# Token mixing: the delta rule's keys ahead of the RWKV solve, gates and values placed around the head norms, and modulation products held back

## The chip, the core and the metric

The kernel runs on one core of a Trainium2 chip, as one program. The metric is the device time of one execution in microseconds (us), lower is better. TensorE (PE) multiplies matrices, VectorE (DVE) and ScalarE (ACT) work elementwise, GpSimd (POOL) runs a small triangular inverse, and SyncE (SP) issues nearly all the DMA transfers.

## The reference, cut to what matters

Two streams of 128 tokens (context and latent) go through two layers with the same weights. A layer is a half-step FFN, token mixing, and a second half-step FFN; each of the three is modulated by shift, scale and gate vectors made from a conditioning vector.

```python
def trunk_layer(x, mod, lp, init, ctx_kv, rope):
    m = mod[:, None]
    h = adaln(x, lp["norm_g"][0], m[:, :, 0], m[:, :, 1])
    x = x + 0.5 * m[:, :, 2] * swiglu(h, lp["ffn_w_in"][0], lp["ffn_w_out"][0])
    h = adaln(x, lp["norm_g"][1], m[:, :, 3], m[:, :, 4])
    y, aux = token_mixing(h, lp, init, ctx_kv, rope)
    x = x + m[:, :, 5] * y
    h = adaln(x, lp["norm_g"][2], m[:, :, 6], m[:, :, 7])
    x = x + 0.5 * m[:, :, 8] * swiglu(h, lp["ffn_w_in"][1], lp["ffn_w_out"][1])
    return x, aux
...
def token_mixing(h, lp, init, ctx_kv, rope):
    pa, pb, pc, pd, pg = split_last(h @ lp["w_in"], BLOCK_SIZES)
    y_a, st_a = rwkv7_mixer(pa, lp, init[0])
    y_b, st_b = gla_mixer(pb, lp, init[1])
    y_c, st_c = delta_mixer(pc, lp, init[2])
    ...
    up = jnp.einsum("bsmc,mcd->bsmd", branches, lp["w_branch"])
    gates = jax.nn.sigmoid(pg.reshape(b, s, N_BRANCH, D_MODEL))
    merged = jnp.sum(gates * up, axis=2)
    return merged @ lp["w_out"], (st_a, st_b, st_c, k, v)
```

RWKV and the delta rule are recurrences over the tokens, written as unit-triangular systems of 128 rows for 4 heads, 2 directions and 2 streams. Both end with a norm over the 64 values of each head, as does GLA.

## The kernel before, in words

All weights are float32 and stream from HBM. `wload` brings a piece of up to 512 KB into one of three `raw` buffers (a DMA on SP's queue), and `part` splits each half of it into a high part (`hi`, on ACT) and a low part (`lo = raw - hi`, on DVE), each in one of four buffers. A matrix product is then three fast products: `lo` times the high part of the activations, `hi` times their high part, `hi` times their low part. One split piece of 512 columns feeds 12 TensorE instructions in the mixing, and `block` chains these so that nothing comes between them unless a scheduler needs to.

`mixing` runs the steps that the string `ORDER` names. `b`*mj* is a block: branch *m* (0 RWKV, 1 GLA, 2 delta rule, 3 attention), column block *j* of four. A block is a gate (`gate`: 48 instructions `pg<-h`, four split pieces, then a tanh on ACT) and a value (12 instructions `pu<-yy`, one split piece, which needs the branch's finished output `yy`), then two DVE instructions that multiply and add into `merged` (`mg`). `g2`*j* is a gate of the delta rule's branch alone, kept in an SBUF tile (named g in the trace), and `u2`*j* the value that goes with it. A number behind a colon moves a step ahead in the scheduler's priority. The scheduler sets the final order on every engine; each engine then runs its instructions in that order and waits in place.

The two triangular systems are solved in the same way. A front step fills the system (`SA` for RWKV, `SD` for the delta rule: one tile tag, `S`, with one buffer, so that the second starts when the first is read out). `gather` copies its 32x32 diagonal blocks to `GB` and by DMA to memory (`d<-GB`); `inverse` (`invA`, `invC`) brings them back (`Lb<-d`), inverts them on GpSimd in 62 instructions (`itmp`, `Tb`), and sends the result through memory once more (`d<-Tb`, `TA<-d`); `inverse_out` (`outA`, `outC`) transposes half of it on DVE (`TB<-TA`). `solve`, inside `rwkv_back` and `delta_back`, is four rounds of small TensorE products into `sv` (32 with `TA`, `TB`, then 32 with the system), with ACT or DVE between them, so the scheduler lets gates run in the gaps. `delta_back` then makes the output `yC`, and `headout` norms it: squares on ACT (`hsq`), sums on TensorE (`phs`), a reciprocal root by 11 tiny DVE instructions (`nr`), a broadcast on TensorE (`phr`), then scaling on DVE and the split into `yy`.

`merge_out` splits `merged` into `gg` and multiplies by `w_out` (192 instructions `po<-gg`). The modulation vectors are products `acc<-mraw` (`mod_part`), 64 TensorE instructions in the trace for one vector set; the set for the last gate (`queue_mixing`) is loaded when `u20` starts, into tiles that are free by then, and its products go wherever the scheduler puts them. In the second FFN, `adaln` (`rstd`) squares and sums `xT` (`pss`), takes the root on DVE (`nr`), broadcasts it (`prs`), and makes the next activations `h`.

Of the kernel before, what the change touches and what calls it, by code (L numbers as in the profile page):

```python
# [33 lines left out]
def constants():  # L34
# [52 lines left out]
NEG = CONSTB.shape[1] - 256  # L87


ORDER = """proj_a rwkv_front:-100 proj_t gla_pre proj_d:100 proj_b attention proj_c invA b33 b30 outA rwkv_back:180  # L90
    delta_front invC b31:50 b32 gla:400 b01:-200 b02 b00 b03 b11 b12 b13 b10 outC delta_back g20 g21 u20 g22 u21
    g23 u22:800 u23"""
SPLIT = 40
BLOCK = 1000000
CP = "vavavaavavpa"
# [7 lines left out]
class Net:  # L103
    def __init__(self, ctx, tc, ia, oa, dbg=None):
        self.tc, self.nc, self.ia, self.oa, self.dbg = tc, tc.nc, ia, oa, dbg or {}
        nc = self.nc
        E = ctx.enter_context
        self.cp = E(tc.tile_pool(name="cp", bufs=1))
        self.raw = E(tc.tile_pool(name="raw", bufs=RAW_BUFS))
        self.hl = E(tc.tile_pool(name="hl", bufs=HI_BUFS))  # L110
        self.hp = E(tc.tile_pool(name="hp", bufs=1))
        self.ad = E(tc.tile_pool(name="ad", bufs=1))
        self.sm = E(tc.tile_pool(name="sm", bufs=2))
        self.ps = E(tc.tile_pool(name="ps", bufs=2, space=PSUM))
        self.pw = E(tc.tile_pool(name="pw", bufs=2, space=PSUM))
        self.py = E(tc.tile_pool(name="py", bufs=2, space=PSUM))
        self.mr = None
        self.ch = 0
        self.dr = E(tc.tile_pool(name="dr", bufs=2, space=DRAM))
        cst = self.cp.tile([128, CONSTS.shape[1]], F32, name="cst")  # L120
        self.cst = cst
        self.C = {k: cst[:, o:o + n] for k, (o, n) in COFF.items()}
        self.wg = self.cp.tile([128, CONSTB.shape[1]], BF16, name="wg")
        self.ident = self.C["ident"]
        self.ones = self.cp.tile([128, 128], F32, name="ones")
        nc.gpsimd.memset(self.ones, 1.0)
        self.zb = self.cp.tile([1, 128], BF16, name="zb")
        nc.gpsimd.memset(self.zb, 0.0)
        self.cols = {}
        self.npad = 0  # L130
        self.los = []
        self.pads = [self.ad.tile([128, 2, 2, 130], F32, name=f"pad{i}") for i in range(2)]
        for pad in self.pads:
            nc.gpsimd.memset(pad[:, :, :, 0:1], 0.0)
            nc.gpsimd.memset(pad[:, :, :, 129:130], 0.0)
# [35 lines left out]
    def mm(self, out, lhsT, rhs, start, stop):  # L171
        return self.nc.tensor.matmul(out, lhsT, rhs, start=start, stop=stop)  # L172

    def block(self, mms):


        last = None
        for args in mms:
            self.tc.cur_priority -= BLOCK if last else 0
            i = self.mm(*args)  # L180
            self.tc.cur_priority += BLOCK if last else 0
            if last:
                self.after(i, last)
            last = i

    def tr(self, out, in_):
        p0 = in_.base_partition()
# [42 lines left out]
    def gemm(self, outs, wview, nkc, x, ncol=256, segs=None):  # L230

        nm = (ncol + 127) // 128
        step, sub = 1024 // ncol, 512 // ncol
        wide = isinstance(outs, list)
        for k0 in range(0, nkc, step):
            nk = min(step, nkc - k0)
            if segs is None:  # L240
                srcs = [(0, wview[:, k0:k0 + nk, :])]
            else:
                srcs = [(o, wview[:, k0:k0 + nk, c0:c0 + n]) for o, c0, n in segs]
            part = self.wload(srcs, nk, ncol)
            for kk in range(0, nk, sub):
                n2 = min(sub, nk - kk)
                wh, wl = part(kk, n2)
                mms = []
                for m in range(nm):
                    o = outs[m][:, 0:256] if wide else outs[:, m * 256:(m + 1) * 256]  # L250
                    first, last = (0, nm - 1) if not wide else (m, m)
                    sl = slice(m * 128, (m + 1) * 128)
                    for k in range(n2):
                        kc = k0 + kk + k
                        start, stop = kc == 0 and m == first, kc == nkc - 1 and m == last
                        if wide:
                            two = [(o, wl[:, k, sl], x[:, kc, 0], False, False),
                                   (outs[m].rearrange("p (a t) -> p a t", a=2), wh[:, k, sl], x[:, kc], start, stop)]
                            mms += two[::-1] if start else two
                        else:  # L260
                            mms.append((o, wl[:, k, sl], x[:, kc, 0], start, False))
                            mms.append((o, wh[:, k, sl], x[:, kc, 0], False, False))
                            mms.append((o, wh[:, k, sl], x[:, kc, 1], False, stop))
                self.block(mms)

    def halves(self, out, ps):

# [48 lines left out]
    def mod_part(self, tiles, l, v):  # L316


        w = self.ia["w_mod"][l].rearrange("(k p) c -> p k c", p=128)
        raws, acc = {}, []  # L320

        def load(k):
            raws[k] = tiles()
            c0 = v * 1024
            for t in raws[k]:
                n = t.shape[1]
                self.nc.sync.dma_start(out=t, in_=w[:, k, c0:c0 + n])
                c0 += n

        def prod(k):  # L330
            if k == 0:
                acc.append(self.py.tile([128, 256], F32, tag="y", name="acc"))
            raw = raws.pop(k)
            n = 1024 // len(raw) // 256
            self.block([(acc[0][32 * j:32 * j + 32], self.cT[:, k, :], raw[j // n][:, 256 * (j % n):256 * (j % n) + 256],
                         k == 0, k == 7) for j in range(4)])

        def last():
            row = self.sm.tile([128, 256], F32, tag="mrow", name="modrow", bufs=2)
            self.act(row, acc[0], AF.Copy)  # L340
            p = self.py.tile([128, 256], F32, tag="y", name="acct")
            for c in range(2):
                self.tr(p[:, c * 128:(c + 1) * 128], row[:, c * 128:(c + 1) * 128])

            x = p.rearrange("p (c j e) -> p j c e", c=2, j=4)[:, :, :, 0:2]
            b = self.bm[l][:, 8 * v:8 * v + 8].rearrange("p (j c) -> p j c", j=4).unsqueeze(3)
            o = self.mod[l][:, 8 * v:8 * v + 8, :].rearrange("p (j c) e -> p j c e", j=4)
            for e in range(2):
                self.tt(o[:, :, :, e:e + 1], x[:, :, :, e:e + 1], b, ALU.add)

        return [partial(load, k) for k in range(8)], [partial(prod, k) for k in range(8)] + [last]
# [21 lines left out]
    def flush(self):  # L373

        if self.mr is not None:
            self.fill(len(self.loads), len(self.prods))
            self.mr.close()
            self.mr = None

    def modcols(self, l, i):  # L380

# [157 lines left out]
    def mixing(self, l):  # L539
# [4 lines left out]
        self.mx = self.mr.enter_context(self.tc.tile_pool(name="mx", bufs=1))  # L544
        self.merge_start(l)
        self.first = set(range(4))
        self.g2 = []
        for step in ORDER.split():
            step, _, ahead = step.partition(":")
            ahead = int(ahead or 0)  # L550
# [373 lines left out]
    def rwkv_back(self, l):  # L924
        C = self.C
# [15 lines left out]
                    self.state_out(p, self.oa["o_rwkv"][l, d])  # L941
        self.mm(self.yA, self.zb, self.wg[0:1, 0:512], False, True)

        y = self.t("m1", [128, 512], name="ysA", bufs=2)
        self.act(y, self.yA, AF.Copy)
        p = self.wkt()
        self.mm(p, C["bo"], y, True, True)
# [17 lines left out]
        self.Y[m] = yy  # L965


    def delta_front(self, l):
        nc, ia, C = self.nc, self.ia, self.C
        P, dv = self.P[l]  # L970
        QC = self.QC
# [25 lines left out]
        be = self.t("be", [128, 2, 8])  # L997
# [21 lines left out]
        ev = eg.rearrange("p (d c t) -> p d c t", d=2, c=2)  # L1019
        for d in range(2):  # L1020
            self.tt(EK[:, d], KQ[:, 1], ev[:, d].unsqueeze(2).to_broadcast([128, 2, 2, 128]), ALU.mult)
        self.yC = self.py.tile([128, 512], F32, tag="y", name="yC")
        self.mm(self.yC, self.zb, self.wg[0:1, 0:512], True, False)
        self.SD = SD = self.t("S", [128, 4, 2, 4, 128], name="SD")
# [2 lines left out]
        for s in range(2):  # L1027
# [24 lines left out]
            if s == 1:  # L1052
                for d in range(2):
                    self.gather(SD, d)
            for d in range(2):
                U = UD[:, 2 * d + s].rearrange("p h v -> p (h v)")
                if s == 0:
# [255 lines left out]
    def branch(self, l, m, j, part):  # L1313

        if part == "g":
            if j % 2 == 0:
                self.g2 += [self.t("ab"[j // 2] + "4", [128, 4, 256], name="g2")]
            self.gate(m, j, self.g2[j // 2][:, 2 * (j % 2):2 * (j % 2) + 2])
            return
        if part == "u":  # L1320
            if j == 0:
                self.queue_mixing(l)
            th = self.g2[j // 2][:, 2 * (j % 2):2 * (j % 2) + 2]
        else:
            th = self.t("th", [128, 2, 256], bufs=2)
            self.gate(m, j, th)
# [21 lines left out]
    def merge_out(self, l):  # L1348
# [5 lines left out]
        for k, n in OUT_UNITS:  # L1354
            p = self.mmt("po")
            self.gemm(p, wo[:, :, 128 * k:128 * (k + n)], 8, gg, ncol=128 * n)
            self.residual(p, k, n, ga)


    def finish(self):  # L1360
# [114 lines left out]
```

## Time and profile before

| | |
|---|---|
| median of 3 runs | 1620.99 us (1619.61 to 1624.06) |
| profiled execution | 1624.48 us, its span 1622.7 us |
| mean granted TensorE clock | 0.977 |
| TensorE busy | 1559.8 us, 96% of the span |
| VectorE, ScalarE, GpSimd busy | 1118.9, 871.1, 168.8 us |
| read from HBM | 303.87 MB, 190 GB/s over the span |

The span runs from the first to the last instruction; 1.8 us of the execution lie around it. Matmuls are pipelined, so a busy TensorE is not one at its peak: the start-to-start distances say more. The granted clock is 1.00 at 2.4 GHz and 0.50 at 1.2 GHz, its two levels. The mixing of the first layer lies at about 250 to 625 us, that of the second at about 1045 to 1417 us.

### The profile page before, as it was taken

The numbers are of one execution on the slowest core, as the hardware profiler recorded it, in microseconds if no ns is written. First come the engines' busy times: TensorE is split into PE (matmuls) and PEld (weight loads), VectorE is DVE, ScalarE is ACT, GpSimd is POOL, SyncE is SP. The second block draws the span as 40 slices with busy tenths as digits, with TensorE's granted clock in tenths as the row PEclk, the third lists the DMA queues.
The fourth block names the chain that finished last, engine by engine and source line by source line (L and its number), as shares of the span: only waits on it lengthen the run. The fifth ranks groups of instructions, "written<-read, shape, count | busy, mean of one in ns | idle before, by whom it ended". The sixth has DMA issues, their size and how long they took to land.

```text
span 1622.7 us, 30913 instructions
## 1 busy us (share of the span) xinstructions
PE 1559.8 (96%) x11760; PEld 1335.7 (82%) x11760; DVE 1118.9 (69%) x2478; ACT 871.1 (54%) x1737; POOL 168.8 (10%) x332
## 2 busy tenths in 40 slices
PE   6999999999999989999999999999999988999997
PEld 3888888888878878888878888888887887988886
DVE  4667667777687358777577775777857853877765
ACT  3556556556444346666456665554644443666653
POOL 0000000153018000000000000002800450000000
PEclk9999999999999899999999999999999998999999
DMA  9899776445246445996779867563544562646653
GB/s 341 303 316 314 247 246 200 105 111 150 75 118 190 114 127 180 314 311 199 234 234 317 277 205 227 181 175 79 144 120 117 144 169 66 186 147 188 194 184 115
DMA packets 276996, 310.86 MB, mean 192 GB/s; under 512 B 23792, under 2 KB 254192, under 8 KB 276848
## 3 DMA queue, kind: packets, MB, share of 16 engines
q1 hardware_dynamic: 274832, 302.60, 59.4%
q0 software_dynamic: 1728, 5.24, 1.6%
q8 instruction: 92, 1.51, 0.4%
q10 hardware_dynamic: 288, 1.05, 0.2%
q14 instruction: 56, 0.46, 0.1%
HBM read 303.87 MB, written 4.98 MB: 190 GB/s over the span
## 4 chain that ended last, share of the span: by engine, by line
PE 80%; DVE 7%; POOL 5%; DMA 4%; issue 2%; ACT 2%; SPq 0%; DVEq 0%; ACTq 0%; POOLq 0%
PE pg L172 21%; PE po L172 18%; PE pu L172 16%; PE acc L172 4%; PE wk L172 4%; PE pA L172 4%; PE sv L172 3%; POOL Tb L881 2%; POOL itmp L880 2%; DVE lo L160 2%; PE pT L172 1%; PE yA L172 1%; PE phs L172 1%; DMA TA<-d 1%; PE phr L172 1%
## 5 line engine op out<-in xcount | busy, mean ns | idle before, releaser
L160 DVE TENSOR_TENSOR lo<-raw,hi 128x512 fp32r<-128x512 f32 (+2 forms) x840 | 576.0, 692 | 290.9 <-ACT hi L157 287.0
L157 ACT ACTIVATE hi<-raw 128x512 fp32r<-128x512 f32 (+2 forms) x840 | 520.5, 625 | 451.7 <-PE pg L172 140.1
L172 PE MATMUL pg<-h,hi 128*128 128x256 f32 (+1 forms) x1728 | 444.9, 334 | 6.6 <-DVE h L163 3.6
L172 PE MATMUL pg<-h,lo 128*128 128x256 f32 x1216 | 339.5, 291 | 0.8 <-ACT hi L157 0.5
L172 PEld LDWEIGHTS pg<-h,hi 128*128 128x128 f32 x1728 | 294.6, 194 | 36.3 <-issue 5.4
L172 PEld LDWEIGHTS pg<-h,lo 128*128 128x128 f32 x1216 | 234.8, 193 | 19.9 <-issue 4.9
L172 PE MATMUL po<-zz,hi 128*128 128x512 f32 x704 | 247.5, 396 | 0.0
L172 PE MATMUL pu<-h,hi 128*128 128x512 f32 x704 | 247.4, 396 | 0.0
L172 PE MATMUL po<-zz,lo 128*128 128x256 f32 x704 | 193.1, 282 | 0.0
L172 PE MATMUL pu<-h,lo 128*128 128x256 f32 x704 | 181.6, 278 | 0.0
L172 PEld LDWEIGHTS po<-zz,hi 128*128 128x128 f32 x704 | 130.8, 188 | 30.9 <-issue 0.8
L172 PEld LDWEIGHTS pu<-h,hi 128*128 128x128 f32 x704 | 129.3, 188 | 24.0 <-issue 0.4
L172 PEld LDWEIGHTS pu<-h,lo 128*128 128x128 f32 x704 | 132.4, 188 | 7.7
L172 PEld LDWEIGHTS po<-zz,lo 128*128 128x128 f32 x704 | 132.1, 188 | 2.9 <-DVE gs L163 0.4
L205 POOL COPY GB<-SA 32x128 f32<-32x128 f32 x16 | 4.7, 294 | 879.4 <-ACT SA L157 879.0
L172 PE MATMUL acc<-mraw,cT 128*32 128x256 f32 x1152 | 83.1, 418 | 8.7 <-DMA mraw<-in_w_mod 8.6
L881 POOL TENSOR_TENSOR Tb<-Tb,itmp 128x126 f32<-128x126 f32 (+22 forms) x124 | 67.9, 548 | 9.7
L172 PEld LDWEIGHTS acc<-mraw,cT 128*32 128x32 f32 x1152 | 35.3, 117 | 40.6 <-issue 13.2
L880 POOL TENSOR_TENSOR itmp<-Lb,Tb 128x126 f32<-128x126 f32 (+22 forms) x124 | 64.2, 518 | 27.0 <-DMA Lb<-d 17.6
L172 PE MATMUL pA<-h,hi 128*128 128x256 f32 x320 | 57.7, 283 | 0.0
L172 PEld LDWEIGHTS pA<-h,hi 128*128 128x128 f32 x320 | 49.9, 192 | 0.0
L172 PE MATMUL pu<-yy,hi 128*128 128x256 f32 x256 | 48.1, 283 | 0.3 <-DVE yy L160 0.3
(343 smaller groups left out, 2272.8 us busy)
## 6 DMA issues: line engine op xcount, KB each, us to landing
raw<-in_ffn_w_in SPq DMA_DIRECT2D x176, 512.0 KB, 4.3
mraw<-in_w_mod SPq DMA_DIRECT2D x138, 512.0 KB, 6.1
raw<-in_w_in SPq DMA_DIRECT2D x106, 512.0 KB, 3.9
raw<-in_ffn_w_out SPq DMA_DIRECT2D x76, 512.0 KB, 4.2
raw<-in_w_branch SPq DMA_DIRECT2D x32, 256.0 KB, 3.5
raw<-in_w_out SPq DMA_DIRECT2D x16, 512.0 KB, 4.1
raw<-in_ffn_w_out SPq DMA_DIRECT2D x12, 256.0 KB, 3.0
raw<-in_ffn_w_out SPq DMA_DIRECT2D x8, 384.0 KB, 4.1
```

The source lines that it names most:

```text
L157: self.nc.scalar.activation(out, in_, func, bias=bias, scale=scale, **kw)
L160: return self.nc.vector.tensor_tensor(out, a, b, op)
L172: return self.nc.tensor.matmul(out, lhsT, rhs, start=start, stop=stop)
L205: (self.nc.vector if eng == "v" else self.nc.gpsimd).tensor_copy(out, in_)
L880: nc.gpsimd.tensor_tensor(tv, a, b, ALU.mult)
L881: nc.gpsimd.tensor_tensor(T[:, 0:n, j + 1:32], T[:, 0:n, j + 1:32], tv, ALU.subtract)
```

## The change

`delta_front` is cut in three: `delta_keys` (norms, keys, decays) runs ahead of the three attention blocks that stand before the RWKV solve, `delta_systems` (filling `SD`, the gathers) right behind `rwkv_back`, and `delta_rhs` after the inverse is issued. The three late attention blocks come in another order. For GLA's first blocks, two gates are made ahead (`h11`, `h12`, kept in `th`) and their values after (`v11`, `v12`). `b10` moves behind `delta_back`, and the four gates `g2` come before the four values `u2`. The modulation products of the last gate are chained behind the last product of `merge_out` (`hold`). The RWKV output's copy `ysA` gets another tile.

```diff
-ORDER = """proj_a rwkv_front:-100 proj_t gla_pre proj_d:100 proj_b attention proj_c invA b33 b30 outA rwkv_back:180
-    delta_front invC b31:50 b32 gla:400 b01:-200 b02 b00 b03 b11 b12 b13 b10 outC delta_back g20 g21 u20 g22 u21
-    g23 u22:800 u23"""
+ORDER = """proj_a rwkv_front:-100 proj_t gla_pre proj_d:100 proj_b attention proj_c invA delta_keys b33 b30 b31 outA
+    rwkv_back:180 delta_systems:180 invC b32 delta_rhs gla:400 b01:-200 b02 b00 b03 h11 h12 v11 v12 b13 outC delta_back
+    b10 g20 g21 g22 g23 u20 u21 u22 u23"""
...
-    def block(self, mms):
+    def block(self, mms, hold=None):
...
-            if last:
-                self.after(i, last)
+            if last or hold:
+                self.after(i, last or hold)
             last = i
+        return last
...
-                self.block(mms)
+                self.big = self.block(mms)
...
             self.block([(acc[0][32 * j:32 * j + 32], self.cT[:, k, :], raw[j // n][:, 256 * (j % n):256 * (j % n) + 256],
-                         k == 0, k == 7) for j in range(4)])
+                         k == 0, k == 7) for j in range(4)], self.hold)
...
-            self.mr = None
+            self.mr = self.hold = None
...
-        y = self.t("m1", [128, 512], name="ysA", bufs=2)
+        y = self.t("e4", [128, 512], name="ysA")
...
+        self.dk = S0, KQ, EK, VC, be, gl
+
+    def delta_systems(self, l):
+        nc, C = self.nc, self.C
+        S0, KQ, EK, VC, be, gl = self.dk
         self.yC = self.py.tile([128, 512], F32, tag="y", name="yC")
...
+    def delta_rhs(self, l):
+        S0, KQ, EK, VC, be, gl = self.dk
+        UD = self.UD
+        for s in range(2):
             for d in range(2):
...
+        if part == "h":
+            th = self.hs[j] = self.t("th", [128, 2, 256], bufs=2)
+            self.gate(m, j, th)
+            return
...
+        elif part == "v":
+            th = self.hs.pop(j)
...
             self.residual(p, k, n, ga)
+        self.hold = self.big
```

Three places show what the scheduler makes of it. The first is TensorE at the end of the delta rule in the first layer, where `yC` is finished and its norm begins. Before:

```order
L172 MATMUL yC<-SD,UD 64x128 x4
L172 LDWEIGHTS zb
L172 MATMUL yC<-wg,zb 128x512
L172 MATMUL phs<-cst,hsq 128x2 x4
L172 MATMUL phr<-cst,nr 64x128 x8
L172 MATMUL acc<-mraw,cT 32x256 x16
```

And now, from the same product on:

```order
L173 LDWEIGHTS zb
L173 MATMUL yC<-wg,zb 128x512
L173 MATMUL pg<-h,lo 128x256
L173 MATMUL pg<-h,hi 128x256 x2
L173 MATMUL pg<-h,lo 128x256
L173 MATMUL pg<-h,hi 128x256 x2
```

Gate products have come in: 12 `pg` between the solve's last round and `yC`, 12 between `yC` and `phs`, 36 between `phs` and `phr`, and 96 behind `phr`, where the 16 rows of `acc` stood (a row of `acc` is two instructions in the trace). The second layer reads the same.

The second place is TensorE between `merge_out` and the second FFN, first layer. Before:

```order
L172 MATMUL pss<-ones,ssq 128x1 x4
L172 MATMUL pss<-ones,sq 128x1 x2
L189 MATMUL acct<-cst,modrow 128x128 x2
L172 MATMUL pss<-ones,sq 128x1 x2
L172 MATMUL prs<-cst,nr 128x128 x2
L172 MATMUL pg<-h,hi 128x512
```

Now:

```order
L173 MATMUL pss<-ones,ssq 128x1 x4
L173 MATMUL pss<-ones,sq 128x1 x2
L173 MATMUL acc<-mraw,cT 32x256 x12
L173 MATMUL pss<-ones,sq 128x1 x2
L173 MATMUL acc<-mraw,cT 32x256 x16
L173 MATMUL prs<-cst,nr 128x128 x2
L173 MATMUL acc<-mraw,cT 32x256 x4
L173 MATMUL pg<-h,hi 128x512
```

All 32 rows of `acc` have moved into this stretch, the transpose `acct` behind it.

The third place is VectorE at the merge of the first layer, from the first value of the delta rule's branch to the splits of `merged` (g is a kept gate, `mg` is `merged`, `gg` its low part). Before, its second half:

```order
L163 SCALAR_TENSOR_TENSOR g_6823<-g_6823,pu 128x512
L160 TENSOR_TENSOR lo<-raw,hi 128x512
L160 TENSOR_TENSOR mg<-mg,g_6823 128x512
L160 TENSOR_TENSOR lo<-raw,hi 128x512
L163 SCALAR_TENSOR_TENSOR g_6823<-g_6823,pu 128x512
L160 TENSOR_TENSOR gg<-mg,gg 128x2x256
L160 TENSOR_TENSOR mg<-mg,g_6823 128x512
L160 TENSOR_TENSOR lo<-raw,hi 128x512 x2
L160 TENSOR_TENSOR gg<-mg,gg 128x2x256
```

Now, all four values:

```order
L164 SCALAR_TENSOR_TENSOR g_6639<-g_6639,pu 128x512
L161 TENSOR_TENSOR lo<-raw,hi 128x512
L161 TENSOR_TENSOR mg<-mg,g_6639 128x512
L164 SCALAR_TENSOR_TENSOR g_6639<-g_6639,pu 128x512
L161 TENSOR_TENSOR lo<-raw,hi 128x512
L161 TENSOR_TENSOR mg<-mg,g_6639 128x512
L164 SCALAR_TENSOR_TENSOR g_6780<-g_6780,pu 128x512 x2
L161 TENSOR_TENSOR mg<-mg,g_6780 128x512 x2
L161 TENSOR_TENSOR lo<-raw,hi 128x512
L161 TENSOR_TENSOR gg<-mg,gg 128x2x256 x4
```

Before, two of the four `gg` were made while gates still ran on TensorE, and the other two stood among the last values; now all four stand behind the last value. On TensorE the four values are 48 instructions in a row, with the 192 of `po<-gg` right behind.

Between the last filling product of `SD` (`pg<-delta`) and the first product of the delta solve, TensorE had 312 `pg`, 84 `pu` and 32 `acc` (as the trace counts) in each layer; now it has 300 and 84 in the first and 264 and 72 in the second, no `acc`, and in both more of GLA's small products: in the first 12 `wk<-wg,la`, 40 `pc`, 6 `wk<-zqq,Z` and 22 others, in the second 12, 32, 6 and 20.

## Rows read from the trace of the kernel before

**Rows 1.** The page, busy time and share of the span by engine.

```profile
PE 1559.8 (96%) x11760; PEld 1335.7 (82%) x11760; DVE 1118.9 (69%) x2478; ACT 871.1 (54%) x1737; POOL 168.8 (10%) x332
```

**Rows 2.** TensorE's waits, whole span: us in total, times, longest.

```profile
PE sv L172 <- DVE TB L890: 8.7, 4, 3.8
```

**Rows 3.** TensorE's waits from 480 to 545 us.

```profile
PE sv L172 <- DVE TB L890: 3.3, 1, 3.3
```

**Rows 4.** TensorE's waits from 569 to 581 us.

```profile
PE phr L172 <- DVE nr L163: 2.4, 1, 2.4
PE yC L172 <- ACT UD L157: 1.3, 1, 1.3
PE phs L172 <- ACT hsq L157: 0.7, 1, 0.7
```

**Rows 5.** Windows: us, then busy time per engine, granted clock, DMA share, GB/s.

```profile
470.00:480.00 10.00, 10.00 (x69) 7.60 (x68) 9.77 (x32) 4.26 (x8) 1.92 (x6) 1.00 0.17 53
540.00:550.00 10.00, 9.48 (x77) 8.80 (x78) 4.79 (x9) 1.80 (x3) 0.00 (x0) 0.50 0.29 79
550.00:560.00 10.00, 10.00 (x107) 9.48 (x108) 4.12 (x7) 3.55 (x6) 0.00 (x0) 0.84 0.19 56
570.00:580.00 10.00, 6.16 (x61) 5.05 (x63) 3.06 (x14) 2.46 (x6) 0.00 (x0) 0.86 0.42 129
...
1190.00:1200.00 10.00, 10.00 (x130) 8.95 (x129) 6.12 (x14) 4.44 (x8) 0.00 (x0) 1.00 0.36 98
```

**Rows 6.** Chain that ended last, 560 to 605 us: start, us, what.

```profile
578.77 1.97 PE phr L172 x16
580.74 3.46 PE acc L172 x32
...
586.29 5.29 PE pg L172 x44
```

**Rows 7.** The same chain, 245 us.

```profile
243.25 1.86 PE acc L172 x32
```

**Rows 8.** The same chain, between merge and second FFN, first layer.

```profile
624.71 1.23 PE pss L172 x12
...
628.85 1.24 PE prs L172 x4
...
631.87 6.28 PE pg L172 x25
...
645.08 5.63 PE pg L172 x32
```

**Rows 9.** VectorE's timeline at the merge, first layer: start, us, instruction.

```profile
601.50 0.69 DVE L160 TENSOR_TENSOR lo<-raw,hi 128x512 fp32r<-128x512 f32 x1
602.13 0.69 DVE L163 SCALAR_TENSOR_TENSOR g<-g,pu 128x512 f32<-128x512 f32 x1
602.74 0.69 DVE L160 TENSOR_TENSOR gg<-mg,gg 128x512 fp32r<-128x512 f32 x1
```

**Rows 10.** The same chain, values and small products, second and first layer.

```profile
1193.76 1.41 PE pu L172 x12
...
467.61 0.25 PE pc L172 x8
467.86 0.76 PE wk L172 x3
```

**Rows 11.** The same chain from filled system to solve, both layers.

```profile
476.23 1.67 DVE SD L160 x5
...
484.33 4.26 DMA Lb<-d
...
532.20 7.63 DMA TA<-d
...
540.52 1.91 PE sv L172 x32
...
1275.77 6.67 DMA Lb<-d
...
1326.92 4.46 DMA TA<-d
```

More of the change, by code (lines that the diff above doesn't have):

```diff
@@ L131, in __init__ @@
         self.los = []
+        self.hold = None
         self.pads = [self.ad.tile([128, 2, 2, 130], F32, name=f"pad{i}") for i in range(2)]
@@ L546, in mixing @@
         self.first = set(range(4))
-        self.g2 = []
+        self.g2, self.hs = [], {}
         for step in ORDER.split():
@@ L965, in ymix, with delta_keys @@
         self.Y[m] = yy
-    def delta_front(self, l):
+    def delta_keys(self, l):
         nc, ia, C = self.nc, self.ia, self.C
```

## The prediction

> **What bounds the kernel now.** The page's busy times come first: TensorE is busy for 96% of the span, VectorE for 69%, so at first sight only about 63 us are left on TensorE [rows 1]. Two things are hidden in that. The list of TensorE's waits shows where it really stands still; the largest is the first product of a triangular solve, which waits for the transposed inverse four times, 8.7 us in all [rows 2], and 3.3 of it is the delta rule in the first layer [rows 3] (3.8, the longest, is the same place in the second layer; the two RWKV solves share the other 1.6). At the end of the delta rule three waits stand one behind the other: 1.3 for the solve's last copy, 0.7 for the squares of the head norm, 2.4 for its root [rows 4]; the second layer has the same three. The windows then show what no wait shows: from 540 to 560 us the granted clock is 0.50 and 0.84, and from 570 to 580 it is 0.86, each time right after such a wait [rows 5]. The level is 1.2 GHz there, and TensorE counts as busy while it does its work at half speed. So the kernel is bound by TensorE's work plus its waits plus the half-clock stretches behind them, and I sum these three over the mixing of both layers. Work that only changes place cancels.
>
> **The change part by part.** The sum is made against the profiled execution (1624.5 us) and moved to the median of the three runs (1621.0), 3.5 lower. 0.3%, 4.9 us, is about what a measurement of this kernel can tell from no change.
>
> *End of the delta rule.* 12, 12 and 36 gate products now stand in the three waits. 44 of them take 5.29 us, 0.12 each [rows 6], so 1.4, 1.4 and 4.3 us of work cover 1.3, 0.7 and 2.4 us. Their inputs depend on nothing in this branch, and 96 more behind `phr` cover the scaling and the split of the output. Gain 4.4 a layer, 8.8. `phr` ran at half clock for 1.97 us [rows 6] and should take half of that: another 1.0 a layer, 2.0. If the cover failed, both would be nothing.
>
> *Held products.* `acc` of 32 instructions takes 1.86 us at full clock [rows 7] and took 3.46 behind `phr`, at half clock [rows 6]. Removing 64 a layer frees 3.7 plus those 1.6. They now lie in the stretch before the second FFN, which lasts from 624.71 to 631.87, 7.2 us [rows 8]: 1.2 of sums, a root that ends at 628.85, and 3.0 from the broadcast to the first gate. Now 24 `acc` (1.4) stand ahead of the last sums, 32 (1.9) beside the root, 8 beside the making of `h`. By this row order: 1.2 + 1.4 + 0.5 + 2.2 + 3.0 = 8.3 us, so the stretch grows by 1.2. In return the clock should hold: the first 25 FFN products took 6.28 us, while 32 take 5.63 a little later [rows 8], so 25 are worth 4.4 and 1.9 was lost. The three other norms of this kind have 128 `acc` in them, and their products behind run at full speed. Per layer −3.7 −1.6 +1.2 −1.9 = −6.0, both −12.0. If the clock falls all the same, −8.2.
>
> *Merge.* This is a new wait. VectorE's 512-wide instructions start 0.61 us apart [rows 9]. From the end of the first value, the third order excerpt has twelve of them up to the first `gg`: four multiplications of gate and value, four `mg`, three `lo`, one `gg`. 12 x 0.61 = 7.3, with 0.2 for the handing over 7.5 us. TensorE needs 3 x 1.41 us for the other three values [rows 10] and 0.24 to the product that reads `gg`: 4.5. It stands for 3.0 us with nothing behind that could go first, since its order is fixed. Nothing in the trace says whether the clock falls after one such wait in dense work; after the waits above it fell for several us, which costs half their length. I add 1.7 (between 0 and 3.4) and get 4.7 a layer, +9.4.
>
> *The wait for the inverse.* From the last system blocks on VectorE (476.23) to the solve (540.52) a chain of transfers and GpSimd runs for 64.3 us [rows 11] that TensorE can't shorten; it waits when its own work ends sooner. By the counts above that work changes in the first layer by −12 `pg` (1.4), −32 `acc` (1.9) and +80 small products. At 0.03 for a `pc` and 0.25 for a `wk<-wg,la` [rows 10], and 0.05 to 0.25 for the others, these are 7.7, together +4.4. The wait of 3.3 goes. In the second layer it is −48 `pg` (5.8), −12 `pu` (1.4), −32 `acc` (1.9) and +7.1, or −2.0, and the wait grows from 3.8 to 5.8. Sum −1.3. The transfers inside differ by 2.4 (`Lb`) and 3.2 us (`TA`) from layer to layer [rows 11], in opposite directions, so the bounds are 3 us either way in each.
>
> With the first layer's wait its half-clock stretch should go. The windows lose 5.0 and 1.6 us to it, 6.6 [rows 5]. The nearest rows are the RWKV solves, which have the same products: in the second layer, after about 1 us of waiting, the clock stayed at 1.00 [rows 5]; in the first, after 0.6, it was low for 3.4 us, a loss of 1.7 or so. I take −4.6, between 0 and −6.6. In the second layer it stays.
>
> The Trainium skill (TensorE: Matmul & The Clock Gate, section A second HAM failure mode: psum-queue depth-cycling) speaks against that gain: TensorE may lose its clock through many tiny idles between groups of matmuls, with no long wait; by it the sum would lack the 4.6. The RWKV solve at 1190 us, at full clock [rows 5], does not agree.
>
> *Ahead of the RWKV solve* the keys and one more block stand in front of the first product, so that its inverse is there in time. But these short waits (1.6 in both layers) go back to weights that land late, and may move instead of going. I take −1.0, between 0 and −3.
>
> *The systems* now follow RWKV's norm at once. VectorE has 75 instructions from that norm to the second gather, by shape 15 of 512 columns, 24 of 256 (0.33 each, as five `SD` show [rows 11]) and 36 small, some 25 us; while it filled the systems before, it was busy 9.77 of 10 us [rows 5], with no wait on TensorE, as gates stood between. Now there are 48 gate products and 12 value products. I add 1.0 a layer, +2.0 (0 to 4 each).
>
> Moving `delta_rhs`, `ysA` and GLA's pairs of gates costs nothing: 96 products (11 us) cover GLA's norm as before, and each moved instruction still runs once. The DMA issues on SP change order, not number; before `u20` the vectors load as early as before, with no one waiting.
>
> Sum: −8.8 −2.0 −12.0 +9.4 −1.3 −4.6 −1.0 +2.0 = −18.3. The profiled execution would be 1606.2; from the median, **1603 us**.
>
> **The rivals.** (a) *The merge is hidden*: no wait, −9.4 more, 1593. For it: the same splits were hidden before. Against it: half of them no longer lie under gates. (b) *The first layer's solve still waits*, by a longer transfer, and keeps its slow stretch: 3.3 + 4.6 back, 1611. For it: transfers of 4.26 and 6.67 us for the same block [rows 11]. (c) *The systems make VectorE the bound*, slower than before: four rounds of mask, exponential, product and masking hand over between VectorE, TensorE and ScalarE, and TensorE waits in place for each, where gates used to stand. From 9.2 us of it a layer the gain is gone; if 8 of the hand-overs wait 1.3 us, a layer loses 10.4 and 1.7 of clock, and the time is 1603 + 24 − 2 = 1625. Against it: rows with 9.77 busy and no wait. (d) *The moves don't cover*: the gates in the tail lack weights, since the third `raw` buffer comes free late; 4.4 a layer and the clock come back, 1603 + 11 = 1614. (e) *The solve's own rounds lose the clock*: its small products hand over to ScalarE and VectorE four times, and the low stretch of the first layer stays though the first wait is gone: 1603 + 4.6 = 1608. For it: both delta solves ran at half clock. Against it: the second RWKV solve, with the same rounds, did not [rows 5]. It is what the rule of the Trainium skill named above would make here.
>
> **How the numbers follow.** The forecast holds with 0.55, (a) 0.10, (b) 0.12, (c) 0.08, (d) 0.09, (e) 0.06. From 1590, a little below (a), to 1614, (d) and the worse end of (b), all but (c) and some of the edges are in; that is 0.8. The forecast's own range is 1597 to 1609. Below 1616.1 lie the forecast, (a), (b), (e) and most of (d): faster 0.86; within 0.3% 0.07; slower 0.07, nearly all of (c).
>
> **What would show it.** In the tail, `yC`, `phs` and `phr` without a wait over 0.3 us and clock 1.00 from 4 us behind the solve to the merge. At the merge, one wait of about 3 us between the last `pu` and the first `po` in each layer. Before the second FFN 64 `acc`, 8.3 us from the first sum to the first gate, full speed behind it. The delta solve's first wait near 0 in the first layer, near 6 in the second. TensorE's waits between RWKV's norm and the second gather below 2 us. It would be wrong if the merge's wait is hidden, if the solve loses its clock without a wait, or if the systems show waits of several us.

## The result, and the profile after

The changed kernel takes 1605.56 us (median of 6, 1599.26 to 1611.51) against 1620.30 for the kernel before; the ratio is 0.9897, with a 95% interval of 0.9874 to 0.9919 (the quotient of these two medians is 0.9909, or 14.7 us). The forecast was 1603, its range 1590 to 1614. The profiled execution took 1606.15 us, 18.3 less than that of before, which is the predicted sum. That it agrees to the tenth is chance: the six executions lie 12 us apart, with a mean granted clock of 0.989 in the shortest and 0.983 in the longest, and every row below comes from one execution of its kernel. The sum came out right; what some of its parts are worth by themselves did not, as the experiments show.

First the page of the changed kernel, busy time by engine, to be held against [rows 1]:

```profile
PE 1547.1 (96%) x11750; PEld 1325.8 (83%) x11760; DVE 1123.5 (70%) x2478; ACT 868.8 (54%) x1737; POOL 169.1 (11%) x332
```

TensorE's busy time fell by 12.7 us though its work is the same (ten records are missing here): for the most part that is half clock that went. Its share of the span is still 96%, so the share tells nothing. Its waits over the whole span (us in total, times, longest):

```profile
PE po L173 <- DVE gg L161: 5.0, 2, 2.5
...
PE pu L173 <- DVE g L164: 3.2, 2, 1.6
...
PE sv L173 <- DVE TB L892: 2.4, 1, 2.4
PE acct L191 <- ACT modrow L158: 2.3, 5, 0.5
PE pu L173 <- DVE lo L161: 2.0, 1, 2.0
```

The solve's waits for `TB`, 8.7 us four times in [rows 2], are one of 2.4, in the second layer's delta rule. The waits of [rows 4] have left the list. New is `po` for `gg`, and `pu` for a gate tile has grown from 0.6 to 3.2: the merge, once in each layer. The chain that ended last, from the solve's end to the second FFN of the first layer (start, us, what), answers to [rows 6] and [rows 8]:

```profile
562.80 4.41 PE pg L173 x36
567.20 1.02 PE phr L173 x16
...
589.91 0.61 DVE gg L161
590.53 0.04 issue
590.57 23.97 PE po L173 x190
614.54 1.23 PE pss L173 x12
615.77 1.43 PE acc L173 x24
```

36 gate products lie where the root's 2.4 us were, and `phr` takes 1.02 in place of 1.97. At the merge the chain leaves TensorE and runs through VectorE's last `gg`. Before the second FFN TensorE's timeline (start, us, instruction, wait before it) shows what is left of the two waits there, 2.2 and 1.8 before:

```profile
614.38 0.95 PE L173 MATMUL pss<-ones,ssq 128*128 128x1 f32 x8
...
619.96 0.71 PE L173 MATMUL prs<-cst,nr 128*128 128x128 f32 x4 [0.35 <-DVE nr L164]
620.60 0.64 PE L173 MATMUL acc<-mraw,cT 128*32 128x256 f32 x8
622.46 0.47 PE L173 MATMUL pg<-h,hi 128*128 128x512 f32 x1 [1.22 <-DVE h L164]
```

From the first sum to the first gate it is 8.1 us (624.54 to 631.87, 7.3 us, in the same rows of the kernel before). The windows (us, busy time per engine, granted clock, DMA share, GB/s) of both layers, to be held against [rows 5]:

```profile
530.00:540.00 10.00, 10.00 (x108) 9.36 (x109) 5.24 (x8) 3.22 (x7) 0.00 (x0) 0.83 0.56 159
540.00:550.00 10.00, 10.00 (x152) 9.17 (x149) 5.11 (x8) 5.30 (x9) 0.00 (x0) 1.00 0.30 79
550.00:580.00 30.00, 30.00 (x295) 28.27 (x293) 15.30 (x34) 13.78 (x25) 0.00 (x0) 1.00 0.42 125
580.00:590.00 10.00, 6.30 (x50) 5.71 (x48) 7.84 (x14) 5.89 (x10) 0.00 (x0) 1.00 0.66 208
590.00:600.00 10.00, 9.43 (x68) 9.43 (x69) 7.12 (x16) 4.20 (x8) 0.00 (x0) 0.83 0.35 107
600.00:630.00 30.00, 28.35 (x246) 24.38 (x245) 24.37 (x72) 17.44 (x42) 0.00 (x0) 1.00 0.41 124
...
1310.00:1320.00 10.00, 7.64 (x97) 7.05 (x97) 4.91 (x9) 3.55 (x6) 0.79 (x1) 1.00 0.52 132
1320.00:1330.00 10.00, 10.00 (x108) 9.48 (x108) 4.12 (x7) 3.55 (x6) 0.00 (x0) 0.83 0.43 136
```

The tail and the FFN behind the merge run at 1.00. Behind each delta solve's start 3.4 us at 1.2 GHz are left of 13.7, in the second layer too, where TensorE still waits; and 3.4 are new behind each merge. Last, TensorE's waits in the systems' stretch, 436 to 480 us; the kernel before has none there:

```profile
PE pc L173 <- DVE X L161: 1.4, 3, 0.7
PE wk L173 <- DVE gm L161: 0.6, 1, 0.6
PE wk L173 <- DVE Z L161: 0.3, 1, 0.3
PE wk L173 <- DVE Dg L161: 0.3, 1, 0.3
```

### The profile page after: what moved, and what is told of

Same layout as the page of the kernel before. It is cut to its first block, busy times and chain, and to the rows that moved or that the text cites. A ratio compares the mean times of both kernels' runs of the same rounds, so it can differ in the third digit from the quotient of the medians.

```text
span 1604.4 us, 30900 instructions
## 1 busy us (share of the span) xinstructions
PE 1547.1 (96%) x11750; PEld 1325.8 (83%) x11760; DVE 1123.5 (70%) x2478; ACT 868.8 (54%) x1737; POOL 169.1 (11%) x332
## 4 chain that ended last, share of the span: by engine, by line
PE 82%; DVE 8%; DMA 5%; POOL 2%; issue 2%; ACT 1%; SPq 0%; DVEq 0%; ACTq 0%; POOLq 0%
PE pg L173 25%; PE po L173 17%; PE pu L173 17%; PE wk L173 4%; PE pA L173 4%; PE acc L173 3%; PE sv L173 3%; DMA raw<-in_w_in 2%; DMA mraw<-in_w_mod 2%; DVE lo L161 2%; PE pR L173 1%; PE pT L173 1%; POOL Tb L883 1%; POOL itmp L882 1%; PE yA L173 1%
## 5 line engine op out<-in xcount | busy, mean ns | idle before, releaser
L173 PE MATMUL acc<-mraw,cT 128*32 128x256 f32 x1152 | 78.5, 397 | 8.9 <-DMA mraw<-in_w_mod 8.8
L173 PE MATMUL pA<-h,hi 128*128 128x256 f32 x320 | 57.7, 283 | 0.0
L173 PE MATMUL po<-gg,hi 128*128 128x256 f32 x256 | 47.8, 290 | 5.0 <-DVE gg L161 5.0
```

## The experiments

The question was no longer how much, but which part brings it. Ratios are to the kernel before, run on the same chip; intervals are 95%.

**1. The values spread through the gates.** All else as in the changed kernel:

```diff
-    b10 g20 g21 g22 g23 u20 u21 u22 u23"""
+    b10 g20 g21 g22 u20 g23 u21:30 u22 u23"""
```

> The changed kernel, with the last four values spread through the gates: behind phr now 48 gate products, a value, 36, a value, 12, two values, then po. Theory (VectorE's backlog behind four values in a row makes the merge's wait, 1.6 + 0.2 + 2.5 us in the changed kernel, and the low clock of 3.4 us behind it): both go, 4.3 of waits and some 1.2 of clock a layer, about 1595 us, a ratio near 0.983 to the kernel before. Rival (VectorE is the bound of the whole stretch, the values' work now delays the low parts of the gates): the wait only changes its place to the gate products, within 2 us of the changed kernel, a ratio of 0.988 to 0.990.

Measured: 1597.27 us, 0.9848 [0.9822, 0.9874]. TensorE's waits at the first layer's merge, 560 to 610 us:

```profile
PE po L173 <- DVE gg L161: 0.5, 1, 0.5
PE pu L173 <- ACT g L158: 0.3, 1, 0.3
PE po L173 <- DVE g L164: 0.2, 1, 0.2
```

1.0 in place of 4.3, and no low clock there. The theory holds: four values in a row leave VectorE behind, and it costs some 8 us in all by the medians (the two intervals just touch). The rival's waits on gate products do not appear.

**2. The changed kernel without the holding.**

```diff
-        self.hold = self.big
```

> The changed kernel without the chain that holds the modulation products: 48 of the 64 in each layer now stand among the last value and the first po products, in the merge's waits; 16 stay before the second FFN. Theory 1 (as predicted, holding them is worth 6.0 us a layer by itself): 12 us slower than the changed kernel, about 1617, ratio 0.997. Theory 2 (they cost only where nothing waits: at the merge 2.8 us of them cover 2.4 of the 4.3 of waits, the stretch before the FFN gets 0.7 shorter, the FFN's first products lose 1.0 to the clock): 0.7 a layer, about 1607, ratio 0.990 to 0.992.

Measured: 1601.28 us, 0.9879 [0.9850, 0.9908]; the changed kernel's interval overlaps it. TensorE's waits from the merge to the second FFN of the first layer, 570 to 630 us:

```profile
PE prs L173 <- DVE nr L164: 1.8, 1, 1.8
PE pg L173 <- DVE h L164: 1.8, 1, 1.8
PE pu L173 <- DVE g L164: 0.9, 1, 0.9
```

The waits before the second FFN are back, 1.8 for the root and 1.8 for `h`, with 6.8 us at half clock there, and the merge's wait has shrunk from 4.3 to 0.9. The two about cancel. Theory 1's 12 us are excluded, since 0.997 lies outside the interval; the ratio lies below theory 2's range, 0.990 to 0.992, into which the interval reaches. In the second layer 32 of the products stand ahead of the delta solve and 32 at the merge, where 48 at the merge and 16 before the FFN were expected; that solve waits 1.6 us in place of 2.4.

**3. The kernel before with the holding alone.** The hunks of the diff that concern `hold`, in the kernel before.

> The kernel before with the holding of the modulation products alone. Theory 1 (the term as predicted stands by itself): 64 products and their slow clock leave the mixing, 10 to 12 us faster, ratio 0.993. Theory 2 (behind the last phr they covered the making of yy: VectorE finishes yy at 583.85 us, TensorE ends them at 584.13): the first value now waits for yy, some 3 us a layer, at the low clock, and the 1.7 us behind the other phr lengthen the delta solve's wait; within 3 us of the kernel before, ratio 0.998 to 1.002.

Measured: 1620.38 us, 0.9988 [0.9966, 1.0011]. The row that theory 2 needs, whole span:

```profile
PE pu L173 <- ACT yy L158: 9.6, 4, 3.1
```

0.8 us of such waits stood in the kernel before. The held products had covered the making of `yy`, twice in each layer. Theory 1's 0.993 lies outside the interval, and theory 2's range and its waits for `yy` are there. The longer wait at the delta solve came in the second layer only (6.7 us in place of 3.8); in the first it fell from 3.3 to 0.7, with 3.1 us of waiting for `yy` ahead of it. At the end of the delta rule 10.2 us ran at half clock in each layer, where it had been 6.8.

**4. The kernel before with the new end alone.**

```diff
-... b13 b10 outC delta_back g20 g21 u20 g22 u21 g23 u22:800 u23
+... b13 outC delta_back b10 g20 g21 g22 g23 u20 u21 u22 u23
```

> The kernel before with the new order of its end alone: block b10 behind the delta rule, the four gates ahead of the four values. Theory (the gates that cover the tail are taken from ahead of the delta solve, which the earlier systems alone can pay for): the tail's waits go (4.4 a layer, 1.0 of clock on phr), the modulation products lie in the merge's waits (3 a layer gained), but the merge costs 5.5 and the solve's first wait grows from 3.3 and 3.8 to about 10.5 and 11 us a layer: some 4 a layer slower, 1628 us, ratio 1.003 to 1.007. Rival (the terms are independent as in the sum that was predicted: tail -10.8, merge +9.4, products -3): 1616, ratio 0.997.

Measured: 1622.21 us, 1.0009 [0.9994, 1.0024], between the two, and neither's number. The direction of the theory shows in the first layer's solve, 510 to 560 us:

```profile
PE sv L172 <- DVE TB L890: 6.6, 1, 6.6
```

and 8.6 in the second layer. The wait grew by 3.3 and 4.8 us, where 7.2 were expected in each: the gates in the tail are paid for ahead of the solve. The rest of the 7.2 is for the most part the chain itself: from the last start of `SD` to that of `TB` it took 57.7 us in the first layer, where the kernel before took 61.5, and 60.2 for 61.8 in the second. At the merge, with the modulation products in it, `pu` waits 0.8 and 1.0 us.

**5. The front alone.** The changed kernel with the end as before and without the holding:

```diff
-    rwkv_back:180 delta_systems:180 invC b32 delta_rhs ... v11 v12 b13 outC delta_back
-    b10 g20 g21 g22 g23 u20 u21 u22 u23"""
+    rwkv_back:180 delta_systems:180 invC b32 delta_rhs ... v11 v12 b13 b10 outC delta_back
+    g20 g21 u20 g22 u21 g23 u22:800 u23"""
```

> The changed kernel with the end of the mixing as before (b10 ahead of the delta solve, values between the gates) and without the holding: what is left is the front, the delta rule's keys and systems early and GLA's pairs of gates. Theory 1 (the front is worth what the prediction gave it: solve's wait -1.3, its clock -4.6, RWKV -1.0, systems +2.0): 4.9 us faster than before, ratio 0.997. Theory 2 (the systems are filled 15 us earlier, TB is there 13 us earlier, and with b10 left ahead of the solve TensorE has about 7 us of work more than the chain: both delta solves lose their first waits of 3.3 and 3.8 and most of the low clock behind, 5 to 6 us each, for 3 us of new waits in the systems): 14 to 17 us faster, ratio 0.990; the front carries nearly the whole gain.

Measured: 1606.28 us, 0.9915 [0.9890, 0.9940], which is 13.8 us and excludes the 4.9 of theory 1; theory 2's 0.990 lies inside. No solve waits for `TB`. The instructions that fill `SD` and that transpose `TB`, first layer (last columns: first and last start in us):

```profile
L892 DVE STREAM_TRANSPOSE TB<-TA x1: 443/443/443, 533.6 to 533.6; 128x256 f32<-128x256 f32 x1
...
L161 DVE TENSOR_TENSOR SD<-pg,dm x16: 410/412/417, 453.1 to 462.7; 128x256 f32<-128x256 f32 x16
```

The same row of the kernel before:

```profile
L160 DVE TENSOR_TENSOR SD<-pg,dm x16: 412/413/418, 467.2 to 478.5; 128x256 f32<-128x256 f32 x16
```

There the last `SD` starts 15.8 us later, and the solve waited until 540.52 [rows 11]. Here the solve starts at 537.2, and `TB` has been there for 3 us. The room is larger than that, since the transfer that brings the inverse had landed earlier:

```profile
L887 POOL DMA_DIRECT2D TA<-d x1: 1194/1194/1194, 520.8 to 520.8; - x1
...
DMA to landing us min/median/max: 5.4/5.4/5.4
```

It landed at 526.2 (520.8 and 5.4), and VectorE made `TB` 7.4 us later, behind other work in its order. With 0.4 us for the transpose the inverse could have been there at 526.6, some 10 us before TensorE came to the solve; in the second layer (landed at 1314.5, solve at 1320.2) it is 5 us.

**6. Each quarter of `merged` split at once.** In `branch`, behind the last addition; `merge_out` keeps only the products:

```diff
+        if part == "u":
+            if j == 0:
+                self.gg = self.t("S", [128, 8, 2, 256], F32R, name="gg")
+            self.split(self.gg[:, 2 * j:2 * j + 2, 0], self.gg[:, 2 * j:2 * j + 2, 1], mg)
```

> The changed kernel with each quarter of merged split as soon as it is summed, so that VectorE makes gg behind each mg and not all four behind the last; TensorE's order stays. Theory 1 (the order on VectorE makes the wait): the first po finds its gg, and only VectorE's 18 instructions of 0.61, 10.9 us, against TensorE's 9.9 to the last quarter are left: the merge's waits fall from 4.3 to 1.0 to 2.6 us a layer, with some clock 3 to 8 us faster than the changed kernel, ratio 0.985 to 0.988. Theory 2 (VectorE's load alone makes it): the wait moves to later po products and stays at 4 us, ratio 0.989 to 0.990.

Measured: 1599.19 us, 0.9866 [0.9841, 0.9892]. The merge's waits, 570 to 600 us:

```profile
PE pu L173 <- DVE g L164: 1.4, 1, 1.4
PE po L173 <- ACT hi L158: 0.8, 1, 0.8
PE po L173 <- DVE gg L161: 0.2, 1, 0.2
```

2.4 in place of 4.3, and no low clock behind. The rows are theory 1's. The ratio is inside its range, but the interval reaches into theory 2's too.

**7. The first and the sixth together.**

> Values spread through the gates (the first experiment) and the early splits together. If the first experiment's spread has taken all of the merge's wait, nothing is left to gain: ratio 0.984 to 0.986, no wait at po. If VectorE was still late for gg there: up to 2 us better, 0.983.

Measured: 1596.09 us, 0.9841 [0.9815, 0.9867], the first experiment's number again. In the first layer `po` waits for 0.2 us.

**8. The sixth, with `b10` back ahead of the delta solve.**

```diff
-... v12 b13 outC delta_back b10 g20 g21 g22 g23 ...
+... v12 b13 b10 outC delta_back g20 g21 g22 g23 ...
```

> The early splits, with b10 back ahead of the delta solve and the four values in a row. The tail keeps 48 gate products between the last round and phr, and 36 behind phr (7 us less). If the second layer's delta solve still waits because too little work lies ahead of it (2.4 us for TB in the changed kernel), that wait goes, with up to 2 us of clock, the first layer is unmoved: about 4 us better than the run with early splits alone, ratio 0.983 to 0.985. If the wait there is only given back at the first value (yy late behind 36 gates) or at the merge: no better than the run with early splits alone.

Measured: 1592.28 us, 0.9826 [0.9801, 0.9851]: the lowest median here, ahead of both kernels (its interval lies clear of the changed kernel's, and overlaps those of experiments 1, 6, 7 and 9). The second layer's solve no longer waits, and the windows behind it show full speed, where 0.83 stood above:

```profile
1310.00:1320.00 10.00, 10.00 (x118) 9.48 (x117) 5.67 (x9) 4.39 (x8) 0.00 (x0) 1.00 0.59 175
1320.00:1330.00 10.00, 10.00 (x142) 9.24 (x141) 4.13 (x6) 5.15 (x9) 0.00 (x0) 1.00 0.33 99
```

The wait is gone in the ninth experiment too, which has the same `ORDER`. The full speed is not: there 3.4 us at half clock lie behind each delta solve.

**9. The eighth without the holding.**

> The fastest kernel so far (early splits, b10 ahead of the solve) without the holding: 24 modulation products stand at the merge, where TensorE waits 0.8 and 0.2 us a layer, 32 stay before the second FFN, 8 go elsewhere. Theory 1 (holding is worth what was predicted, 6.0 a layer): 12 us slower, ratio 0.990. Theory 2 (it only moves work between places that wait a little): the stretch before the FFN gets about 0.7 shorter and keeps 32 products beside the root, the merge grows by 1.0 a layer; within 3 us of that kernel, ratio 0.981 to 0.985.

Measured: 1595.79 us, 0.9830 [0.9802, 0.9858], the same within the intervals, and theory 1's 0.990 lies outside. Theory 2, for the second time, though not by its counts: 32 of the products stand at the merge in each layer, and the other 32 before the second FFN in the first layer and ahead of the delta solve in the second.

**10. The front alone with the keys late.** Against the fifth:

```diff
-invA delta_keys b33 b30 b31 outA rwkv_back:180 delta_systems:180
+invA b33 b30 b31 outA rwkv_back:180 delta_keys:180 delta_systems:180
```

> The front alone, but with the delta rule's keys behind the RWKV solve, at the systems' priority; the systems, the gathers and the rest stay early. Theory 1 (the early keys bring the front's gain: with them late the systems are filled some 15 us later and only 45 us of work by the order's counts are left to cover the chain of 61 us from the filled systems to TB): the delta solve waits again, 5 us or more in each layer, with a low clock of 10 us or more behind it; ratio 0.998 or above. Theory 2 (filling the systems ahead of everything else is enough, the keys are short): most of the gain stays, ratio 0.991 to 0.994.

Measured: 1636.65 us, 1.0089 [1.0061, 1.0117]. The filling of the systems, first layer:

```profile
L161 DVE TENSOR_TENSOR SD<-pg,dm x16: 410/411/420, 475.9 to 485.6; 128x256 f32<-128x256 f32 x16
```

TensorE's wait at the solve, 500 to 600 us:

```profile
PE sv L173 <- DVE TB L892: 7.6, 1, 7.6
```

And the windows around it:

```profile
540.00:550.00 10.00, 6.18 (x53) 5.79 (x54) 4.71 (x8) 1.81 (x3) 0.08 (x1) 0.53 0.38 107
550.00:560.00 10.00, 10.00 (x88) 9.48 (x88) 2.75 (x4) 1.95 (x4) 0.00 (x0) 0.62 0.14 41
```

Theory 1 holds. Moving one step, the keys, is worth 28 us on top of the other moves of the front (0.9915 against 1.0089, of 1620). Filled 22.9 us later, the systems leave 7.6 us of waiting in the first layer and half clock for 17.1 us, and 7.7 and 13.6 us in the second. The moved blocks without early keys are worse than no change. Early keys without the other moves were not run.

## Why the prediction was right, and where it was not

*End of the delta rule*, predicted −10.8. The rows agree in every part: three waits gone, `phr` at 1.02, clock 1.00. But the cover is not free. By itself the new end changes nothing that can be told (1.0009): it takes one block, `b10`, from ahead of the solve, and what it gains it loses there, where 3.3 and 4.8 us of waiting are added (experiment 4).

*Held products*, predicted −12.0. This is the step that failed: "removing 64 a layer frees 3.7 plus those 1.6". By the rows of the changed kernel one gets −10.6 (a layer 3.7, 1.6, less 0.8 of longer stretch, and 0.8 for the first 25 FFN products, which take 5.3 us to the next start in place of 6.1), and that reading is wrong as a cause. Removed from the old end, the products leave a wait for `yy` (experiment 3); left in the new one, they fill the merge's wait (experiments 2 and 9). The 1.6 were not theirs either: without them the old end ran 10.2 us at half clock in place of 6.8, so the slow stretch stays behind the waits, whatever stands in it. Holding them is worth nothing that these runs can tell, in the old end at most 5.5 us (0.9966). I had checked what lay behind them, and not which wait they were covering.

*Merge*, predicted +9.4. The mechanism is right. The waits are 1.6, 0.2 and 2.5, 4.3 us a layer in place of 3.0, and the fourth value already waits for VectorE's multiplication of an earlier one. The sum had VectorE busy without a pause, and it is not (VectorE's timeline of the changed kernel, first layer):

```profile
581.72 0.68 DVE L164 SCALAR_TENSOR_TENSOR g<-g,pu 128x512 f32<-128x512 f32 x1
583.76 0.69 DVE L161 TENSOR_TENSOR lo<-raw,hi 128x512 fp32r<-128x512 f32 x1 [1.36 <-ACT hi L158]
584.37 0.68 DVE L161 TENSOR_TENSOR mg<-mg,g 128x512 f32<-128x512 f32 x1
584.97 0.68 DVE L164 SCALAR_TENSOR_TENSOR g<-g,pu 128x512 f32<-128x512 f32 x1
```

For 1.36 us it stands before the split of a piece of `w_out` that, by the chain, landed only at 582.99, with the addition and the next multiplication behind it in its order. By an estimate from this pause some 1.3 of the 4.3 are a late weight and not four values in a row. The early splits keep this pause (1.21 us, and a first wait of 1.4, in experiment 6); where it shrank, to 0.26 us in experiment 8, that wait is 0.5. The clock costs 1.7 and 1.1 on `po` (192 in 24.28 and 23.73 us without the wait, 22.6 in the kernel before), so about +11. Experiment 1 gets 8 back.

*The wait for the inverse*, predicted −5.9 with the clock. In the first layer the wait went, as forecast; 3.4 us at half clock stayed, a loss of 1.7, where the term had left 2.0 of 6.6 in. In the second layer the step failed: 5.8 of wait and the whole slow stretch were forecast, 2.4 and 3.4 us at half clock were measured. 2.0 us of late `lo` ahead of it cover a part; and the clock gave back as much as in the first layer, some 5 us, a gain that the sum put at nothing. It more than made up for what the systems and the merge cost more, and it is in part the luck of one execution: in experiments 1, 2, 6 and 7 the same solve, after waits of 1.6 to 2.3 us, has 6.8 to 13.7 us at half clock.

*The systems*, predicted +2.0: 2.6 in the first layer by the rows above, 1.3 against 0.8 in the second, so +3.1, and in the first layer more than the 2 us that were to be the bound. GLA's pairs of gates were to cost nothing; in the first layer a value waits 0.9 us for its kept gate. The *RWKV solves* no longer wait, −1.6 for −1.0.

*The front as a whole* stood in the sum at −4.9, and is worth −13.8 alone. The two numbers fit together once `b10` is counted: my count of the work ahead of the solve charged the loss of `b10`, 7 us a layer, to the front, and it belongs to the end. With `b10` in place the early systems end the waits in both layers, with 10 and 5 us of room (experiment 5); without it the changed kernel has 3 us left in the first layer and waits 2.4 in the second. So the gain hangs on the keys, made ahead of the RWKV solve, which let the chain of [rows 11] start 15 us earlier (experiments 5 and 10); the rest of the change spent this room on covering the tail, and whether it made more than it spent can't be told: 0.9879 with both (experiment 2) against 0.9915, with overlapping intervals.

Of the rivals, (a) and (d) are excluded by the rows, (b) by a `TB` that is there 3 us before the first layer's solve, (c) by 2.6 us of waits. (e) happened in small: in the first layer the solve does lose the clock without a wait, which stood among the signs of being wrong, but for 3.4 us and not for 13.7.

## What to carry to other kernels

Work that lies in front of a waiting instruction may be what makes the wait short: before crediting its removal, ask which late result it covers. Where a chain that nothing shortens (here 58 to 65 us of transfers and GpSimd, from the last filled block to the inverse) ends in a wait, start it earlier before looking for cover at its end. A sum over the parts of a rearrangement can be right while some parts are not worth what their lines say; run the parts alone.

## What the runs showed of the hardware

A solve that starts without a wait loses little of the clock or nothing, and one that had to wait can lose much. In the traces 29 solves started without a wait, in the changed kernel and eight experiments (3 and 4, with shorter waits, not counted): 17 of them had one stretch of 3.4 us at 1.2 GHz, beginning 5.2 to 6.2 us behind their first product, the other 12 none. The same solve falls now on one side, now on the other: the first layer's delta solve has the stretch in the changed kernel, and not in experiment 1. Of the 12 that had waited for 1.6 us or more, in the kernel before and the other runs, all had low stretches, 3.4 to 17.1 us in sum. So the Trainium skill (TensorE: Matmul & The Clock Gate, A second HAM failure mode: psum-queue depth-cycling) fits here in that the clock fell with no long wait, which I had argued against from one solve that kept its clock. That small idles between groups of matmuls did it, as that section has it, no row shows: TensorE counts as busy throughout (530 to 540 us above). Every solve with more than 3.4 us of it had waited.

In the middle of dense products, at the merge, waits of 1.6, 0.2 and 2.5 us one shortly behind the other came with 3.4 us at half clock in both layers; where they were 1.4, 0.8 and 0.2 us (experiment 6), the clock stayed at full speed.
